# Sums of the down weights formed in the first up projection, with loads and stores on GpSimd's queue

## The chip, the cores and the metric

The kernel runs on one core of a Trainium2 chip. The metric is the device time of one execution in microseconds (us), and each change is judged by the ratio of the medians of timed runs. The engines are named as in the profile: PE is TensorE (matmuls; PEld its weight loads), DVE is VectorE, ACT is ScalarE, POOL is GpSimd, SP is SyncE, whose queue carries most DMA transfers.

## The reference

Two transformer blocks run one after the other on x of 1024 tokens by 1024 features, in float32. Each ends with a feed-forward part of 2816 hidden features:

```
gate, up = jnp.split(xn @ w_gate_up, 2, axis=-1)            # first block
x = x + (jax.nn.silu(gate) * up) @ w_down

u = causal_dwconv(h @ w_ffn_up, w_ffn_conv)                 # second block
gate, val = jnp.split(u, 2, axis=-1)
x = x + (jax.nn.silu(gate) * val) @ w_ffn_down
```

The change is in these two parts. What lies ahead of them (attention, gating, delta rule, short convolutions) is not touched.

## The kernel before

**Precision.** Each float32 operand is split into a high part (ScalarE casts it, line 256) and a low part (VectorE subtracts the high part, line 257). A product is three matmuls: high x high, high x low, low x high.

**Up projection** (`unit`, line 1061). One pass of Strassen's scheme in Winograd's form replaces eight block products by seven. A unit `f` (1 to 21) makes 128 gate and 128 up features: 84 matmuls of 128x512. Its weights come as two raw blocks `wr` and go through four slots (`add_unit`), in which the sums S1 to S4 of weight blocks are formed in place: S3 and S4 on VectorE, S1 and S2 on GpSimd (table `SE`). `unit` copies the first product out of PSUM into a buffer `u` on ScalarE (line 1072); the results go to DRAM as `hd`, feature by feature, through the buffer `sg`.

**Down projection** (`strassen` in `ffn`, line 1231). The same scheme over 20 of the 22 hidden blocks, as two halves of ten: seven products of 10 steps each (`DOWN`: A11 B11, A12 B21, S3 T3, A22 T4, S1 T1, S2 T2, S4 B22), so 70 steps of 12 matmuls. A is the hidden activations read back from `hd`, B the down weights. The two blocks left over go through `down`, which in the first block stands ahead of product S2. Operand `i` is split into one of `AR` = 3 ring buffers `ah` (`operand`), and its sums of A blocks are formed at the same place. B11, B12 and B21 lie whole in SBUF, B22 comes twice through `wr`, and `add_down` forms T1 to T4 from them in the slots: T3 and T1 on VectorE, T2 and T4 on GpSimd (line 845).

**Order.** Each engine works through its instructions in order. A list scheduler sets that order: it may move instructions ahead that it takes to be ready, and operands are issued with a priority (`PR["op"]`). `Weights` keeps up to two raw blocks loaded and three slots split ahead of TensorE; it works through its slots in the order in which they were added.

Of the kernel before, what the change touches and what calls it, by code (L numbers as in the profile page):

```python
# [8 lines left out]
F32 = mybir.dt.float32  # L9
# [9 lines left out]
P = 128  # L19
# [33 lines left out]
DE = dict(S3=pool_, T3=vec_, T1=vec_, T2=pool_, T4=pool_, S1=vec_, S2=vec_, S4=pool_)  # L53
# [104 lines left out]
class Kern:  # L158
# [6 lines left out]
    def setup(self):  # L165
# [5 lines left out]
        self.hd = self.dram.tile([NF, P, S], F32, name="hd")  # L171
        self.ident = c.tile([P, P], F32, name="ident")
# [643 lines left out]
    def plan_ffn(self, which):  # L816
# [5 lines left out]
        for f in range(1, NF):  # L822
            units[f] = self.add_unit(*[up[:, :, o + f * P:o + (f + 1) * P] for o in (0, DFF)])
# [6 lines left out]
        for _, name in DOWN:  # L830
            if which == 1 and name == "T2":
                rest()
            for k in range(0, ND, 2):
                slots[name, k] = self.add_down(home, name, k, dn)
# [4 lines left out]
    def add_down(self, home, name, k, dn):  # L839

        W, nc = self.W, self.nc
        raw = W.load([(0, dn[:, ND + k:ND + k + 2, 512:])], 2, 512) if name in ("T3", "B22") else None

        def tt(out, in0, in1, what):
            DE[what](nc).tensor_tensor(out=out, in0=in0, in1=in1, op=ALU.subtract)  # L845

        def make(hi, lo):
            out = []
            for j in range(2):
                h, l = (v[:, j * 512:(j + 1) * 512] for v in (hi, lo))  # L850
                b11, b12, b21 = (home.get((q, k + j)) for q in ("B11", "B12", "B21"))
                b22 = None if raw is None else W.raw[raw][:, j * 512:(j + 1) * 512]
                if name == "T3":
                    src = home["T3", j]
                    tt(src, b22, b12, "T3")
                    tt(b12, b12, b11, "T1")
                    tt(b11, b22, b12, "T2")
                else:
                    src = dict(B11=b11, B21=b21, T4=b21, T1=b12, T2=b11, B22=b22)[name]
                    if name == "T4":  # L860
                        tt(b21, b21, b11, "T4")
                self.split(h, l, src)
                out.append((h, l))
            return out
        return W.slot(make, raw)

    def add_unit(self, gate, up):
# [9 lines left out]
        def tt(name, in0, in1, op, what):  # L877
            SE[what](nc).tensor_tensor(out=raw(name), in0=raw(in0), in1=raw(in1), op=op)  # L878
# [63 lines left out]
    def ffn(self, which):  # L942
# [118 lines left out]
        def unit(f):  # L1061
# [32 lines left out]

            if f < NF - 1:
                second()
                third()
# [16 lines left out]
            add(u2[:, main], b5, u2[:, main])  # L1114
            if f == NF - 1:
                down_open()
# [19 lines left out]
        def fetch(q, k0, k1):  # L1136

            f = k0 + ND * ((q[2] if q[0] == "A" else q[1]) == "2")
            c = 512 * ((q[1] if q[0] == "A" else q[2]) == "2")
            src = self.hd[f:f + k1 - k0, :, c:c + 512].rearrange("k p c -> p k c") if q[0] == "A" else \  # L1140
                dn[:, f:f + k1 - k0, c:c + 512]
# [9 lines left out]
        def down_load():  # L1151

            for q, part in (("A11", "hi0"), ("B11", "lo0")):
                place(q, self.xnp.tile([P, KT, 512], F32, tag=part, name=q), 0, KT)
            for k in range(0, KT, 2):
                fetch("A11", k, k + 2)
                fetch("B11", k, k + 2)
# [1100 lines left out]
```

## Time and profile before

| what | value |
|---|---|
| median of 3 runs | 2544.11 us (2541.62 to 2544.75) |
| the profiled execution | 2533.62 us |
| its span, first to last instruction | 2531.9 us |
| busy over the span | PE 96%, DVE 73%, ACT 45%, POOL 18% |
| mean granted TensorE clock | 0.986 of full |

The shares are averages over all stages. Where TensorE stands still, and for whom, has to be read stage by stage; the stages of the change lie at 545 to 949.5 us (first up projection), 949.5 to 1189.5 (first down projection, dn1), 1866 to 2285 (second up projection) and 2285.5 to 2524 (second down projection, dn2).

### The profile page before, as it was taken

To read this page: it belongs to the slowest core of one execution; us is meant where nothing else is said; L and a number is where in the kernel's file an instruction comes from. 1 tells how busy PE (TensorE), PEld (TensorE's weight loads), DVE (VectorE), ACT (ScalarE), POOL (GpSimd) and SP (SyncE) were. 2 spreads that over 40 slices of the span, in tenths; PEclk is the share of its full clock that TensorE was granted. 3 is DMA by queue.
4 is the path that set the end of the run, shared out by engine and by line. 5 is a ranking of instruction groups with operands and counts; after the bars stand their busy time and mean duration, and the time that the engine had idled before them with its cause. 6 is when DMAs were issued, how large, how long until landed. Compare 5 with 4: busy or idle time off the path is not lost. (4 is left out here: it accounts for less than half of the span.)

```text
span 2531.9 us, 33317 instructions
## 1 busy us (share of the span) xinstructions
PE 2420.6 (96%) x12360; PEld 1993.5 (79%) x12360; DVE 1856.3 (73%) x3342; ACT 1145.8 (45%) x2290; POOL 449.3 (18%) x412
## 2 busy tenths in 40 slices
PE   7999999999999999899999999989899999999898
PEld 7977779978888887678877777879678888887677
DVE  5557788655555557977777868777878788878977
ACT  5356675342232233337432434776744434434243
POOL 1000002031111114500210111332341111113600
PEclk9999999999999999899999999999999999999999
DMA  4110002112223236213211112131212222227202
GB/s 152 51 34 21 22 26 92 42 48 78 75 83 91 76 110 240 75 42 123 62 42 50 30 46 64 40 137 49 75 51 84 92 75 75 84 93 265 67 33 109
DMA packets 194675, 196.58 MB, mean 78 GB/s; under 512 B 11613, under 2 KB 154032, under 8 KB 194512
## 3 DMA queue, kind: packets, MB, share of 16 engines
q1 hardware_dynamic: 189760, 178.74, 22.2%
q0 software_dynamic: 4752, 15.71, 1.8%
q8 instruction: 97, 1.59, 0.3%
q14 instruction: 66, 0.54, 0.1%
HBM read 155.76 MB, written 38.67 MB: 77 GB/s over the span
## 5 line engine op out<-in xcount | busy, mean ns | idle before, releaser
L257 DVE TENSOR_TENSOR wl<-wr,wh 128x512 fp32r<-128x512 f32 (+4 forms) x388 | 300.9, 805 | 320.1 <-ACT wh L256 316.2
L256 ACT CAST wh<-wr 128x512 fp32r<-128x512 f32 (+4 forms) x388 | 257.2, 696 | 583.4 <-PE st L973 363.9
L269 PE MATMUL dn<-wh,ah 128*128 128x512 f32 x560 | 225.6, 403 | 21.6 <-DVE ah L257 21.6
L267 PE MATMUL dn<-wh,ah 128*128 128x512 f32 x560 | 226.0, 404 | 5.4 <-ACT ah L256 2.2
L268 PE MATMUL dn<-wl,ah 128*128 128x512 f32 x560 | 224.0, 400 | 0.0
L980 DVE TENSOR_TENSOR u<-st,u 128x512 f32<-128x512 f32 x260 | 168.0, 685 | 30.7 <-PE st L973 29.3
L878 POOL TENSOR_TENSOR wr<-wr 128x512 f32<-128x512 f32 x42 | 55.2, 1315 | 692.3 <-DVE wr L878 692.3
L269 PEld LDWEIGHTS dn<-wh,ah 128*128 128x128 f32 x560 | 107.3, 192 | 56.3 <-DVE ah L257 30.8
L973 PE MATMUL st<-f1hi,wl 128*128 128x512 f32 x368 | 147.2, 400 | 0.0
L973 PE MATMUL st<-f2hi,wl 128*128 128x512 f32 x368 | 147.1, 400 | 0.0
L973 PE MATMUL st<-f2lo,wh 128*128 128x512 f32 x368 | 147.0, 400 | 0.0
L973 PE MATMUL st<-f1lo,wh 128*128 128x512 f32 x368 | 146.6, 398 | 0.0
L973 PE MATMUL st<-f1hi,wh 128*128 128x512 f32 x368 | 145.2, 394 | 0.7 <-ACT f1hi L256 0.7
L973 PE MATMUL st<-f2hi,wh 128*128 128x512 f32 x368 | 145.0, 394 | 0.7 <-ACT f2hi L256 0.7
L267 PEld LDWEIGHTS dn<-wh,ah 128*128 128x128 f32 x560 | 107.4, 192 | 32.8 <-ACT ah L256 4.1
L268 PEld LDWEIGHTS dn<-wl,ah 128*128 128x128 f32 x560 | 107.5, 192 | 24.0
L256 ACT CAST ah<-A 128x512 fp32r<-128x512 f32 x104 | 63.7, 619 | 109.7 <-PE dn L268 94.7
L257 DVE TENSOR_TENSOR ah<-A,ah 128x512 fp32r<-128x512 f32 x104 | 82.4, 796 | 41.9 <-ACT ah L256 38.9
L973 PEld LDWEIGHTS st<-f2hi,wh 128*128 128x128 f32 x368 | 70.4, 191 | 17.3 <-ACT f2hi L256 0.9
L973 PEld LDWEIGHTS st<-f1hi,wh 128*128 128x128 f32 x368 | 70.4, 191 | 17.2 <-ACT f1hi L256 0.9
L973 PEld LDWEIGHTS st<-f2lo,wh 128*128 128x128 f32 x368 | 69.6, 189 | 16.0
L973 PEld LDWEIGHTS st<-f1lo,wh 128*128 128x128 f32 x368 | 69.4, 189 | 16.1
(547 smaller groups left out, 7079.8 us busy)
## 6 DMA issues: line engine op xcount, KB each, us to landing
wr<-in_w_gate_up_dram SPq DMA_DIRECT2D x44, 512.0 KB, 4.3
hd<-sg SPq DMA_DIRECT2D x44, 512.0 KB, 3.2
wr<-in_w_ffn_up_dram SPq DMA_DIRECT2D x44, 512.0 KB, 3.9
wr<-in_w_mix_in_dram SPq DMA_DIRECT2D x28, 512.0 KB, 4.0
wr<-in_w_in_dram SPq DMA_DIRECT2D x16, 512.0 KB, 3.9
wr<-in_w_down_dram SPq DMA_DIRECT2D x12, 512.0 KB, 3.3
wr<-in_w_ffn_down_dram SPq DMA_DIRECT2D x12, 512.0 KB, 3.3
A<-hd SPq DMA_DIRECT2D x4, 1280.0 KB, 14.3
```

Source lines behind the costliest of these rows:

```text
L256: self.nc.scalar.copy(hi, src)
L257: self.nc.vector.tensor_tensor(out=lo, in0=src, in1=hi.bitcast(F32), op=ALU.subtract)
L267: mm(out, a[0], b[0], start=start, stop=False)
L268: mm(out, a[0], b[1], start=False, stop=False)
L269: mm(out, a[1], b[0], start=False, stop=stop)
L878: SE[what](nc).tensor_tensor(out=raw(name), in0=raw(in0), in1=raw(in1), op=op)
L973: mm(ps, a[p][:, kk, :], b[q][:, kk, :], start=start and kk == 0 and j == 0, stop=kk == n - 1 and j == 2, skip_group_check=True)
L980: nc.vector.tensor_tensor(out=out, in0=ps, in1=t, op=ALU.add)
```

## The change

- The sums T1 to T4 of both down projections are formed during the first up projection. `prepare_down` goes over 20 blocks (10 of each set of weights): four loads of 128x512 from DRAM, four GpSimd sums, four stores to new DRAM tensors `td`, all on GpSimd's queue. It is a generator which `unit` advances three times, so a unit takes one block. A GpSimd copy of one column from the unit's first result into each load's buffer (`self.now`) ties the loads to the unit.
- In the down projections all seven B operands (four of them from `td`) come through `wr` as blocks of 512 KB for two steps; B11, B12 and B21 no longer lie in SBUF. The loop's own A sum S2 moves from VectorE to GpSimd (`DE`).
- In the first up projection S1 and S2 of the weights move from GpSimd to VectorE (`SE[1]`); in the second they stay.
- The ring of A operands has six buffers, three of them opened when the up projection's pool is released.

```
-ND, AR, A2, PB = 10, 3, 2, 2
+ND, AR, AR0, A2, PB = 10, 6, 3, 2, 2
-SE, TE, ME = dict(S3=vec_, S1=pool_, S2=pool_, S4=vec_), dict(T1=vec_, T2=pool_, T3=pool_, T4=pool_), vec_
+SE = {1: dict(S3=vec_, S1=vec_, S2=vec_, S4=vec_), 2: dict(S3=vec_, S1=pool_, S2=pool_, S4=vec_)}
-DE = dict(S3=pool_, T3=vec_, T1=vec_, T2=pool_, T4=pool_, S1=vec_, S2=vec_, S4=pool_)
+DE = dict(S3=pool_, S1=vec_, S2=pool_, S4=pool_)
...
+    def add_down(self, which, name, k, dn):
+        f, c = k + ND * (name[1] == "2"), 512 * (name[2:] == "2")
+        return self.W.add([(0, dn[:, f:f + 2, c:c + 512] if name[0] == "B" else self.td[which, name][:, k:k + 2, :])],
+                          2, 512)
+    def prepare_down(self, pool):
+        nc = self.nc
+        for which in (1, 2):
+            dn = self.ffn_plan[which][3]
+            for k in range(ND):
+                def load(name):
+                    f, c = k + ND * (name[1] == "2"), 512 * (name[2] == "2")
+                    t = pool.tile([P, 512], F32, tag="pb", name="pb", bufs=6)
+                    nc.gpsimd.tensor_copy(t[:, 0:1], self.now)
+                    nc.gpsimd.dma_start(out=t, in_=dn[:, f, c:c + 512])
+                    return t
+                def keep(name, out, in0, in1, op):
+                    nc.gpsimd.tensor_tensor(out=out, in0=in0, in1=in1, op=op)
+                    nc.gpsimd.dma_start(out=self.td[which, name][:, k, :], in_=out)
+                b12, b22, b11, b21 = (load(n) for n in ("B12", "B22", "B11", "B21"))
+                yield
+                keep("T3", b22, b22, b12, ALU.subtract)
+                keep("T1", b12, b12, b11, ALU.subtract)
+                yield
+                keep("T2", b11, b11, b22, ALU.add)
+                keep("T4", b21, b21, b11, ALU.subtract)
+                yield
...
             nc.scalar.copy(p1[:, main], b1)
+            self.now = p1[:, 2:3]
...
+            next(prep, None)
             if f < NF - 1:
                 second()
+                next(prep, None)
                 third()
...
+            next(prep, None)
             if f == NF - 1:
                 down_open()
...
-            d2 = tc.alloc_tile_pool(name=f"dr{which}", bufs=1, side="right", reuse_waits="tile")
-            dp.append(d2)
+            d = tc.alloc_tile_pool(name=f"dr{which}", bufs=1, side="right", reuse_waits="tile")
+            dp.append(d)
+            ring["ah"] += [d.tile([P, 2, 512], F32R, name=f"ah{i}") for i in range(AR0, AR)]
...
+            for i in range(AR0, AR):
+                operand(i)
```

Three places show how the order moves. The first is GpSimd in the first up projection. Before, it has the two sums S1 and S2 of each unit in the raw blocks `wr`:

```order
L878 TENSOR_TENSOR wr_5970<-wr_5970 128x512 [waits DMAHW2_49,DVE_49,Activation_49]
L878 TENSOR_TENSOR wr_5970<-wr_5970,wr_6053 128x512 [waits DMAHW3_49,Activation_49,Pool_49]
L878 TENSOR_TENSOR wr_6118<-wr_6118 128x512 [waits DMAHW4_49,DVE_49,Activation_49]
L878 TENSOR_TENSOR wr_6118<-wr_6118,wr_6159 128x512 [waits DMAHW6_49,Activation_49,Pool_49]
L878 TENSOR_TENSOR wr_6254<-wr_6254 128x512 [waits DMAHW0_49,DVE_49,Activation_49]
L878 TENSOR_TENSOR wr_6254<-wr_6254,wr_6295 128x512 [waits DMAHW1_49,Activation_49,Pool_49]
```

With the change it has a block of `prepare_down` per unit, here the first one (`pb` are its buffers, `td1T` the DRAM tensors of the first down projection; waits on DMASW are for transfers of its own queue):

```order
L860 COPY pb<-u 128x1 x3
L861 DMA pb<-in_w_down_dram 128x512 [waits DMASW5_49,Pool_49]
L861 DMA pb<-in_w_down_dram 128x512 [waits DMASW6_49,Pool_49]
L861 DMA pb<-in_w_down_dram 128x512 [waits DMASW7_49,Pool_49]
L861 DMA pb<-in_w_down_dram 128x512 [waits DMASW0_49,Pool_49]
L865 TENSOR_TENSOR pb<-pb 128x512 [waits DMASW6_49,DMASW5_49]
L866 DMA td1T_69<-pb 128x512 [waits DMASW1_49,Pool_49]
L865 TENSOR_TENSOR pb<-pb 128x512 [waits DMASW7_49]
L866 DMA td1T_67<-pb 128x512 [waits DMASW2_49,Pool_49]
L865 TENSOR_TENSOR pb<-pb 128x512
L866 DMA td1T_68<-pb 128x512 [waits DMASW3_49,Pool_49]
L865 TENSOR_TENSOR pb<-pb 128x512 [waits DMASW0_49]
```

The sums on `wr` have gone to VectorE, and eight transfers have come.

The second is ScalarE at the start of the first down projection. Before, the rows begin after operands 0 to 2 have been cast, with weight casts (`wh`) and the next operands in the order of the steps (three buffers `ah`):

```order
L256 CAST wh_8838<-B_8777 128x512 [waits DMAHW5_49,DVE_49,PE_49]
L256 CAST wh_8838<-B_8777 128x512
L241 ACTIVATE sg<-u 128x512 [waits DVE_49]
L256 CAST ah_8851<-A_8776 128x512 [waits PE_49,Activation_49]
L256 CAST ah_8852<-A_8776 128x512 [waits DMAHW4_49,PE_49,Activation_49]
L256 CAST wh_8932<-B_8777 128x512 [waits DMAHW7_49,PE_49]
L256 CAST wh_8932<-B_8777 128x512
L256 CAST ah_8853<-A_8776 128x512 [waits PE_49,Activation_49]
```

With the change, the first row is operand 2; the second set of three buffers (`ah_9284` to `ah_9286`) holds operands 3 to 5, and the first set takes operands 6, 7 and 8 (`A11x`):

```order
L260 CAST ah_9256<-A_9184 128x512 [waits DMAHW1_49]
L260 CAST wh_9241<-wr_9219 128x1024 [waits DMAHW4_49,DVE_49,PE_49]
L245 ACTIVATE sg<-u 128x512 [waits DVE_49]
L260 CAST ah_9254<-A_9184 128x512 [waits DMAHW3_49,PE_49,Activation_49]
L260 CAST ah_9255<-A_9184 128x512 [waits PE_49,Activation_49]
L260 CAST wh_9332<-wr_9226 128x1024 [waits DMAHW6_49,PE_49]
L260 CAST ah_9256<-A11x 128x512 [waits DMAHW5_49,PE_49,Activation_49]
L260 CAST ah_9284<-A_9184 128x512 [waits DMASW3_49,DMASW2_49,DMASW4_49,DMASW1_49,Pool_49]
L260 CAST ah_9285<-A_9184 128x512 [waits DMAHW2_49,DMASW3_49,DMASW2_49]
L260 CAST ah_9286<-A_9184 128x512 [waits DMASW3_49]
L260 CAST ah_9284<-A11x 128x512 [waits DVE_49,PE_49]
```

Operands 6, 7 and 8 stand ahead of 3, 4 and 5; the one of step 8 waits for PE to leave its buffer, which holds step 2.

The third is VectorE in the second down projection, where the product S3 T3 is made ready. Before, T3 (`T`) and T1 (`B_20253`) stand among the subtractions of operands (`ah`) and weights (`wl`):

```order
L845 TENSOR_TENSOR T_20244<-wr_20076,B_20253 128x512
L845 TENSOR_TENSOR T_20245<-wr_20076,B_20253 128x512
L257 TENSOR_TENSOR ah_20239<-A_20237,ah_20239 128x512
L257 TENSOR_TENSOR wl_20553<-B_20291,wh_20552 128x512 x2
L845 TENSOR_TENSOR B_20253<-B_20253,B_20164 128x512
L257 TENSOR_TENSOR ah_20240<-A_20237,ah_20240 128x512
L845 TENSOR_TENSOR B_20253<-B_20253,B_20164 128x512
L980 TENSOR_TENSOR x<-dn,x 128x512 x2
L257 TENSOR_TENSOR ah_20238<-A_20237,ah_20238 128x512
L257 TENSOR_TENSOR wl_20593<-T_20244,wh_20592 128x512
```

With the change the same place has only the subtractions, of weights that were read as sums, and the sums into x:

```order
L261 TENSOR_TENSOR ah_20610<-A_20497,ah_20610 128x512
L261 TENSOR_TENSOR wl_20921<-wr_20845,wh_20920 128x1024
L261 TENSOR_TENSOR ah_20611<-A_20497,ah_20611 128x512
L261 TENSOR_TENSOR ah_20612<-A_20497,ah_20612 128x512
L261 TENSOR_TENSOR wl_20959<-wr_20885,wh_20958 128x1024
L261 TENSOR_TENSOR ah_20567<-A_20497,ah_20567 128x512
L990 TENSOR_TENSOR x<-dn,x 128x512 x4
L261 TENSOR_TENSOR ah_20568<-A_20497,ah_20568 128x512
L261 TENSOR_TENSOR wl_20995<-wr_20924,wh_20994 128x1024
L261 TENSOR_TENSOR ah_20569<-A_20497,ah_20569 128x512
```

The VectorE sums of line 845 are gone, and so are those on GpSimd.

## Rows read from the trace of the kernel before

**Rows 1.** Windows of four stages: us, busy us by engine, clock, DMA share, GB/s.

```profile
core 0: us, PE busy (x) PEld busy (x) DVE busy (x) ACT busy (x) POOL busy (x), PEclk, DMA share, GB/s
...
545.00:949.50 404.50, 404.46 (x1743) 328.67 (x1742) 219.92 (x348) 117.21 (x207) 51.70 (x40) 1.00 0.29 86
949.50:1110.00 160.50, 147.71 (x601) 114.98 (x600) 138.77 (x180) 59.65 (x103) 69.52 (x42) 0.96 0.39 141
...
1866.00:2285.00 419.00, 419.00 (x1808) 340.62 (x1807) 338.85 (x510) 175.45 (x324) 51.82 (x40) 1.00 0.26 85
2285.50:2410.00 124.50, 111.71 (x457) 86.52 (x455) 114.44 (x150) 46.58 (x82) 64.86 (x38) 0.97 0.43 157
...
```

**Rows 2.** Tile dn, dn1 then dn2: ns min/median/max, first and last start.

```profile
L267 PE MATMUL dn<-wh,ah x280: 387/397/628, 949.5 to 1189.0; 128*128 128x512 f32 x140
L267 PE MATMUL dn<-wh,hh x32: 388/394/395, 1110.1 to 1131.5; 128*128 128x512 f32 x32
...
L267 PE MATMUL dn<-wh,ah x280: 387/397/628, 2285.5 to 2501.6; 128*128 128x512 f32 x140
L267 PE MATMUL dn<-wh,hh x32: 388/394/395, 2502.3 to 2523.7; 128*128 128x512 f32 x32
```

**Rows 3.** Timeline of TensorE in dn1 and dn2: start us, us.

```profile
949.54 0.39 PE L267 MATMUL dn<-wh,ah 128*128 128x512 f32 x1
...
955.94 0.40 PE L268 MATMUL dn<-wl,ah 128*128 128x512 f32 x1
...
2354.01 0.63 PE L268 MATMUL dn<-wl,ah 128*128 128x512 f32 x1
2354.44 0.63 PE L269 MATMUL dn<-wh,ah 128*128 128x512 f32 x1
```

**Rows 4.** Waits of TensorE, dn1 then dn2: total us, times, longest us.

```profile
PE dn L269 <- DVE ah L257: 10.9, 8, 2.8
...
PE dn L269 <- DVE ah L257: 10.7, 8, 2.9
```

**Rows 5.** Groups by line and shape, 945 to 1150: busy, mean ns, idle before.

```profile
L257 DVE TENSOR_TENSOR wl<-B,wh 128x512 fp32r<-128x512 f32 x44 | 35.8, 853 | 2.9 <-ACT wh L256 2.8
...
L845 POOL TENSOR_TENSOR B<-wr,B 128x512 f32<-128x512 f32 x8 | 18.1, 2261 | 11.6 <-DVE B L845 9.7 <-ACT ah L256 1.9
```

**Rows 6.** The same view of the first up projection, 545 to 950.

```profile
L257 DVE TENSOR_TENSOR wl<-wr,wh 128x512 fp32r<-128x512 f32 x141 | 92.6, 692 | 165.0 <-ACT wh L256 164.2
L256 ACT CAST wh<-wr 128x512 fp32r<-128x512 f32 x141 | 81.6, 618 | 251.8 <-PE st L973 212.3 <-DMA wr<-in_w_gate_up_dram 36.2 <-POOL wr L878 3.4
...
L878 POOL TENSOR_TENSOR wr<-wr,wr 128x512 f32<-128x512 f32 x20 | 25.9, 1294 | 1.6
```

**Rows 7.** Timeline of GpSimd, then VectorE, in dn2.

```profile
2338.33 6.05 POOL L845 TENSOR_TENSOR B<-wr,B 128x512 f32<-128x512 f32 x1
...
2356.58 1.71 POOL L845 TENSOR_TENSOR B<-wr,B 128x512 f32<-128x512 f32 x1
...
2355.40 1.77 DVE L257 TENSOR_TENSOR wl<-T,wh 128x512 fp32r<-128x512 f32 x1
```

**Rows 8.** DMAs issued by line 2141 on GpSimd's queue; their stretch's window.

```profile
L2141 POOL DMA_DIRECT2D xnd<-xs x4: 531/593/604, 1803.2 to 1819.1; - x4
...
DMA to landing us min/median/max: 3.0/3.1/5.7
...
1798.00:1820.00 22.00, 14.50 (x58) 9.03 (x57) 21.38 (x42) 14.64 (x28) 7.72 (x8) 0.80 0.23 89
```

**Rows 9.** Timeline of ScalarE in the first up projection.

```profile
718.59 0.59 ACT L1072 COPY u<-st 128x512 f32<-128x512 f32 x1 [1.27 <-PE st L973]
738.07 0.59 ACT L1072 COPY u<-st 128x512 f32<-128x512 f32 x1 [1.27 <-PE st L973]
```

**Rows 10.** Timeline at dn2's start: TensorE, then the SP queue.

```profile
2289.36 0.50 PE L267 MATMUL dn<-wh,ah 128*128 128x512 f32 x1 [1.61 <-DVE u L980]
...
2296.80 0.33 SPq L1059 DMA_DIRECT2D hd<-sg  x1
```

More of the change, by code (lines that the diff above doesn't have):

```diff
@@ L171, in setup @@
         self.hd = self.dram.tile([NF, P, S], F32, name="hd")
+        self.td = {(w, n): self.dram.tile([P, ND, 512], F32, name=f"td{w}{n}")
+                   for w in (1, 2) for n in ("T1", "T2", "T3", "T4")}
         self.ident = c.tile([P, P], F32, name="ident")
@@ L822, in plan_ffn @@
         for f in range(1, NF):
-            units[f] = self.add_unit(*[up[:, :, o + f * P:o + (f + 1) * P] for o in (0, DFF)])
+            units[f] = self.add_unit(which, *[up[:, :, o + f * P:o + (f + 1) * P] for o in (0, DFF)])
         home, slots = {}, {}
@@ L833, in plan_ffn @@
             for k in range(0, ND, 2):
-                slots[name, k] = self.add_down(home, name, k, dn)
+                slots[name, k] = self.add_down(which, name, k, dn)
         if which == 2:
@@ L837, in plan_ffn @@
         self.ffn_plan[which] = (units, home, slots, dn, dw)
[L839 to L865, printed above, removed]
@@ L869, in add_unit @@
+    def add_unit(self, which, gate, up):
         W, nc = self.W, self.nc
@@ L877, in tt @@
         def tt(name, in0, in1, op, what):
-            SE[what](nc).tensor_tensor(out=raw(name), in0=raw(in0), in1=raw(in1), op=op)
+            SE[which][what](nc).tensor_tensor(out=raw(name), in0=raw(in0), in1=raw(in1), op=op)
         def cut(hi, lo, *names):
@@ L1151, in down_load @@
         def down_load():
-            for q, part in (("A11", "hi0"), ("B11", "lo0")):
-                place(q, self.xnp.tile([P, KT, 512], F32, tag=part, name=q), 0, KT)
+            place("A11", self.xnp.tile([P, KT, 512], F32, tag="hi0", name="A11"), 0, KT)
             for k in range(0, KT, 2):
                 fetch("A11", k, k + 2)
-                fetch("B11", k, k + 2)
         ring = {}
@@ L1165, in down_open @@
             place("A12", d.tile([P, ND, 512], F32, name="A12"), 0, ND)
-            ring["ah"] = [d.tile([P, 2, 512], F32R, name=f"ah{i}") for i in range(AR)]
+            ring["ah"] = [d.tile([P, 2, 512], F32R, name=f"ah{i}") for i in range(AR0)]
             d = tc.alloc_tile_pool(name=f"dm{which}", bufs=1, reuse_waits="tile")
             dp.append(d)
-            for j in range(2):
-                home["T3", j] = d.tile([P, 512], F32, name=f"T3{j}")
             ring["a22"] = [d.tile([P, 512], F32, name=f"a22{i}") for i in range(A2)]
-            for q in ("A11", "B11", "A21", "B12"):
+            for q in ("A11", "A21"):
                 place(q, d.tile([P, ND - KT, 512], F32, name=f"{q}x"), KT, ND)
-            for q, part in (("A21", "hi1"), ("B12", "lo1")):
-                place(q, self.xnp.tile([P, KT, 512], F32, tag=part, name=q), 0, KT)
+            place("A21", self.xnp.tile([P, KT, 512], F32, tag="hi1", name="A21"), 0, KT)
             fetch("A11", KT, ND)
-            fetch("B11", KT, ND)
             fetch("A12", 0, ND // 2)
             fetch("A12", ND // 2, ND)
-            for i in range(AR):
+            for i in range(AR0):
                 operand(i)
@@ L1233, in strassen @@
             last = None
[L1234 to L1235 removed]
+            d = tc.alloc_tile_pool(name=f"dr{which}", bufs=1, side="right", reuse_waits="tile")
+            dp.append(d)
+            ring["ah"] += [d.tile([P, 2, 512], F32R, name=f"ah{i}") for i in range(AR0, AR)]
             self.psum(dn=(1, 8))
[L1237 to L1241 removed]
+            for k0, k1 in ((0, KT // 2), (KT // 2, KT), (KT, ND)):
+                fetch("A21", k0, k1)
             for k in range(A2):
                 load22(k)
+            for i in range(AR0, AR):
+                operand(i)
             sums = []
@@ L1259, in strassen @@
                     banks = [self.bank(tag="dn", name="dn") for _ in range(4)]
-                w = W.get(slots[bname, k - k % 2])[k % 2]
+                w = [v[:, k % 2, :] for v in W.get(slots[bname, k - k % 2])]
                 a = ready.pop(i)
@@ L1282, in strassen @@
                 W.done(slots[DOWN[-1][1], ND - 2])
+                dp.pop(1).release()
             return last
@@ L1287, in ffn @@
         pool = tc.alloc_tile_pool(name=f"ffn{which}", bufs=1, side="right", reuse_waits="tile")
+        prep = self.prepare_down(pool) if which == 1 else iter(())
         first(banks)
@@ L1300, in ffn @@
             down(range(2 * ND, NF), self.tail2())
-            dp[1].release()
+            for d in dp[:0:-1]:
+                d.release()
     def tail1(self):
```

14 lines of the change are left out of this document (3 added, 11 removed).

## The prediction

> **What bounds the kernel now.** I read the busy time by stage first, because the share over the whole span (TensorE 96%) hides where it waits. [Rows 1] has the four stages the change touches. In the first and the second up projection TensorE is busy for all of the stretch (404.46 of 404.5 us, 419.00 of 419) at a granted clock of 1.00: nothing done beside them can make them shorter, only longer. In the first part of each down projection it is not: 147.71 of 160.5 us and 111.71 of 124.5 us, at a granted clock of 0.96 and 0.97, so some of the busy time is slow too. That is where there is time to win.
>
> How much? A step of a down projection is 12 matmuls. Two of them 28 apart start at 949.54 and 955.94 [rows 3], so at the full level (2.4 GHz) one takes 0.2286 us and a step 2.74 us. In the first down projection (dn1 below; the second is dn2) the 50 steps ahead of the two left-over blocks run from 949.5 to 1110.1 [rows 2]: 160.6 us for 600 matmuls that need 137.2, so **23.4 us** are lost. In dn2 all 70 steps run from 2285.5 to 2502.3: 216.8 us for 840 matmuls that need 192.0, so **24.8 us** are lost. Together 48.2 us; the rest of the two stages runs at full pace (so the last 20 steps of the first, whose end also holds tail work, are left out).
>
> Who makes TensorE wait? The chain of waits of these stretches says nearly always the same: the matmul of line 269, which needs the low part of an A operand, waits for the VectorE subtraction of line 257, 8 times and 10.9 and 10.7 us in total [rows 4]. The remainder up to 23 us is the clock: behind such a wait matmuls follow each other by 0.43 us instead of 0.23 [rows 3] (1.2 GHz), after TensorE had stood idle for two or three us.
>
> Why is VectorE late? In that stretch of dn1 it is busy 138.77 of 160.5 us, and its instructions there are longer than elsewhere: the same subtraction of 128x512 takes 853 ns on average in the first down projection [rows 5] and 692 in the up projection [rows 6]. The timeline shows how [rows 7]: while GpSimd forms T2 and T4 (line 845, 1.7 us each, one took 6.05), VectorE's subtractions take 1.77. One VectorE instruction of 0.69 and one GpSimd sum of 1.3 take 1.7 to 1.8 together: they take turns.
>
> **The change, step by step.** (1) *Both down projections* lose ten T3 and ten T1 on VectorE and ten T2 and ten T4 on GpSimd each, and the loads of B11, B12 and B21 in big pieces. Two of the four A sums change engine as well: S2 goes to GpSimd. Per projection VectorE sheds 30 instructions of 0.69 (20 B sums, 10 S2), 21 us, and GpSimd 20 of 1.7 to 2.3 [rows 5, 7] less the ten S2 it takes. What is left for VectorE per step is two subtractions (2 x 0.69), in places a sum for x or S1 (0.69 each): 1.4 to 2.8 us against 2.74 for TensorE. And six operands wait ready in place of three, 16.5 us of work in place of 8.2. So the long waits of the middle should go.
>
> What is late next? Three places. *Step 3.* The order on ScalarE shows that steps 6, 7 and 8 (issued with priority as steps 0 to 2 are consumed) are split ahead of step 3, and step 8 waits until TensorE is done with step 2. So TensorE always stops there once. In dn1 step 2 ends at 949.5 + 36 x 0.2286 = 957.7; then come two casts of 0.62 [rows 6] and a subtraction of 0.69: **2 us**. In dn2 it is longer, as VectorE still has the last convolution: its last product is stored at 2296.80 [rows 10], and behind it come the subtractions of step 7, of two weight blocks (2 x 0.69), of step 8 and step 3: 3.4 us, to 2300.2, where TensorE, which starts again at 2289.36 with 27 matmuls of steps 0 to 2 to go and has two of step 3 that need only the high part, wants it at 2296.0. That is 4 us, and 1.6 for eight matmuls at the lower clock behind it: **5.5 us**. *The start of dn2* keeps most of its wait of 1.61 us [rows 10]: **1 us**. *The A22 product*: GpSimd now has two sums per step there (S2, S4), 2.6 us at 1.29 [rows 6] or 3.4 at 1.7 [rows 7] against a step of 2.74; over eight steps between a lead of 1 us and a lag of 5, and the three more operands cover 8. I keep **2 us** each (0 to 5). Left over: 2 + 2 and 5.5 + 1 + 2, together 12.5; won: 48.2 - 12.5 = **35.7 us**.
>
> (2) *The weight loads in the down projections* become one stream of 512 KB per two steps, 5.5 us. Slots are three deep and raw buffers two, so a load issued as its buffer comes free is wanted two slots, 11 us, later, and a transfer of that size lands in 3.0 to 5.7 [rows 8]. I charge nothing; what covers it is the two slots already split, and without them each late load would cost what it is late.
>
> (3) *The first up projection* gets all the work that was removed. A unit takes 19.48 us (738.07 - 718.59, [rows 9]). VectorE: two sums more per unit, 40 x 0.69 = 28 us, to 248 of 404.5; if all 80 GpSimd sums of 1.3 shut it out, 352, or 87%. In the second up projection VectorE has 338.85 and GpSimd 51.82 of 419, 93%, and TensorE never waits [rows 1]. So the cover is there; without it each unit would lose what VectorE has above 19.48 us. DMA: 160 transfers of 256 KB, 42 MB, bring 86 GB/s at a busy share of 0.29 to about 190 at 0.64; the row of ScalarE's casts says what that may cost: it waits 212.3 us for TensorE to free a slot and 36.2 for weights to land [rows 6], and TensorE for neither. I charge **1 us**.
>
> (4) *GpSimd's block per unit* is the price that nothing in the trace shows whole: four copies of one column, four loads, four sums, four stores. An issue takes 0.53 to 0.60 us, also where VectorE is busy 21.38 of 22 us, and lands 3.0 to 5.7 later [rows 8]; a sum takes 1.29 to 2.26 [rows 5, 6]; a copy of one column lies between nothing and an issue. Low: two issues 1.1, the landing 3.0, then four sums and stores 4 x (1.3 + 0.55): 11.5 us. High: 2.4 + 1.2 + 5.7 + 4 x (2.26 + 0.60): 20.7. I take 14, nearer the low end, since the two sums that GpSimd now has in a unit of this very stage take 1.29 with VectorE busy 54% beside them. Below 19.48 it costs nothing: only ScalarE's copy into `u` of the next unit waits for it, a unit later. The Trainium skill has a rule against transfers on this queue ("SBUF — State Buffer", the section SBUF: two separate sides): while VectorE holds the port that it shares with GpSimd, GpSimd cannot write descriptors, and a DMA of 0.62 us takes some 3.1; it advises another queue. By that rule, if it held for all eight issues, a block would be an estimated 14 + 8 x 2.5 = 34 us and the kernel 290 us slower; by the rows above, 0.53 to 0.60 beside a busy VectorE, nothing.
>
> Sum: 35.7 - 1 = 35 us. The profiled execution took 2533.62 us, 10 less than the median of the runs, 2544.11; I take the difference off the median: **2509 us**.
>
> **Rivals.** *GpSimd cannot do a block per unit.* Then ScalarE's copy waits for it, everything behind that copy on ScalarE too (the casts of weights), and TensorE for these: 20 x (block - 19.48). At the high bound, 20.7, the time is 2533; from 21.2 us on the whole gain is gone; with one sum in each block held up to 6.05 us, as one was [rows 7], on top of the high bound, the block is 24.5 and the time 2609. For it: that row. Against it: it stood where VectorE had no gap, and here VectorE is idle 46% of the time now and 39% with its two sums more. 8%.
> *The up projection loses a little per unit* (weights land late beside 2 MB more per unit, or VectorE's subtractions come late by a GpSimd sum of 1.3): 1 us in each of 20 units gives 2529. 12%.
> *The wait moves within the down projections:* GpSimd's two sums per step in A22, or SP's queue, where weights now stand behind loads that wait for a free buffer, bring back half: 2527. For it: S2 now holds the buffers of A22. 18%.
> *Likeliest*, 62%: 2509, its own range 2499 to 2521 (12.5 left over may be 4 or 22).
>
> **Numbers.** What can be told from no change is 0.2%, 5 us. Faster: all of the likeliest and of the third rival, most of the second, 0.87. Same 0.05. Slower, the first rival with the tail of the second, 0.08. The range is 2497 (nearly all of the loss gone) to 2532, which takes in the second and third rival and leaves out the first.
>
> **What would show it.** Right: 600 and 840 matmuls of dn1 and dn2 in about 142 and 201 us; line 269's wait once per stage near step 3 and hardly elsewhere; VectorE's 128x512 subtractions in the down projections near 0.7; the up projection with TensorE still busy throughout and GpSimd idle for some us of each unit until ScalarE's copy lets it go. Wrong: `u` on ScalarE waiting for GpSimd in the up projection, units longer than 19.5 us, or waits for `a` or `wr` in the middle of the down projections.

## The result, and the profile with the change

The changed kernel takes **2676.07 us** (median of four runs, 2673.15 to 2680.9) against 2542.86 us before: 1.054 times as long, 95% interval 1.0518 to 1.0563. The prediction said 2509.

The windows of the four stages, in the form of [rows 1], say at once where. First up projection, first part of dn1, second up projection, first part of dn2:

```profile
core 0: us, PE busy (x) PEld busy (x) DVE busy (x) ACT busy (x) POOL busy (x), PEclk, DMA share, GB/s
545.00:1108.00 563.00, 451.78 (x1750) 358.64 (x1748) 301.41 (x388) 118.80 (x208) 201.98 (x320) 0.88 0.41 138
1111.00:1255.50 144.50, 141.56 (x599) 113.34 (x600) 117.89 (x123) 57.06 (x80) 53.45 (x31) 0.99 0.48 159
2020.00:2444.00 424.00, 423.22 (x1832) 343.87 (x1833) 343.27 (x514) 178.53 (x329) 54.35 (x42) 1.00 0.26 84
2444.20:2569.00 124.80, 118.70 (x495) 94.78 (x494) 112.51 (x118) 51.66 (x72) 51.94 (x30) 0.97 0.51 170
```

The first up projection, of which TensorE was busy every moment before, takes 563 us in place of 404.5. TensorE stands still in a fifth of it, and its clock is at 0.88 of full. The first row explains the whole result; the down projections did become shorter. Their first and last matmuls, as in [rows 2]:

```profile
L271 PE MATMUL dn<-wh,ah x280: 387/396/628, 1110.9 to 1334.7; 128*128 128x512 f32 x140
L271 PE MATMUL dn<-wh,hh x32: 392/397/398, 1255.8 to 1277.4; 128*128 128x512 f32 x32
...
L271 PE MATMUL dn<-wh,ah x280: 387/396/632, 2444.2 to 2648.5; 128*128 128x512 f32 x140
L271 PE MATMUL dn<-wh,hh x32: 392/394/397, 2649.2 to 2670.7; 128*128 128x512 f32 x32
```

The 50 steps of dn1 take 1255.8 - 1110.9 = 144.9 us (160.6 before), the 70 of dn2 take 205.0 (216.8): 27.5 us won. The spans differ by 2679.0 - 2531.9 = 147.1 us: 157.6 in the units of the first up projection, 0.8 ahead of them, 3.0 between the last matmul of the up projection and the first of dn1, 3.0 behind the last of dn1, less 27.5 in the two products; the other 10.2 lie in stages that the change does not touch. They come from the execution of before that was profiled, which was 9 us faster than the median: with the same code there as before, the last experiment below took 9 us longer between dn1 and the second up projection.

Who makes TensorE wait in the up projection? The waits from 560 to 1060, all engines (us in total, times, longest):

```profile
ACT wh L260 <- DMA wr<-in_w_gate_up_dram: 128.4, 15, 9.4
...
POOL pb L860 <- ACT u L1082: 199.4, 18, 11.8
...
PE st L983 <- DVE u L990: 104.5, 18, 7.0
```

TensorE waits for a VectorE sum, once in each unit, 5.8 us on average. GpSimd waits too: 11 us in each unit for ScalarE's copy `u`, that is, it has done its block well before the next one may start. So the prediction's first rival (GpSimd cannot do a block per unit) is not what happened. ScalarE waits 128 us for weights to land.

### The profile page after: what moved, and what is told of

It is laid out like the page before. It is cut to its first block, busy times and chain, and to the rows that moved or that the text cites. A ratio compares the mean times of both kernels' runs of the same rounds, so it can differ in the third digit from the quotient of the medians.

```text
span 2679.0 us, 33648 instructions
## 1 busy us (share of the span) xinstructions
PE 2466.3 (92%) x12360; PEld 2030.3 (76%) x12360; DVE 1906.1 (71%) x3254; ACT 1139.9 (43%) x2220; POOL 564.0 (21%) x670
## 5 line engine op out<-in xcount | busy, mean ns | idle before, releaser
L261 DVE TENSOR_TENSOR wl<-wr,wh 128x512 fp32r<-128x512 f32 (+3 forms) x438 | 422.6, 988 | 424.5 <-ACT wh L260 420.8
L260 ACT CAST wh<-wr 128x512 fp32r<-128x512 f32 (+3 forms) x438 | 319.1, 755 | 807.0 <-PE st L983 362.0
L983 PE MATMUL st<-f1hi,wh 128*128 128x512 f32 x368 | 165.5, 450 | 111.2 <-DVE u L990 109.2
L983 PEld LDWEIGHTS st<-f1hi,wh 128*128 128x128 f32 x368 | 80.7, 220 | 138.0 <-ACT sg L245 117.0
L983 PE MATMUL st<-f1lo,wh 128*128 128x512 f32 x368 | 162.0, 440 | 0.0
L983 PE MATMUL st<-f1hi,wl 128*128 128x512 f32 x368 | 161.1, 438 | 0.0
L865 POOL TENSOR_TENSOR pb<-pb 128x512 f32<-128x512 f32 x80 | 103.3, 1291 | 95.9 <-DMA pb<-in_w_down_dram 49.2
L261 DVE TENSOR_TENSOR ah<-A,ah 128x512 fp32r<-128x512 f32 x104 | 84.6, 826 | 35.8 <-ACT ah L260 35.7
L888 POOL TENSOR_TENSOR wr<-wr 128x512 f32<-128x512 f32 x21 | 27.2, 1294 | 346.4 <-DVE wr L888 346.4
L983 PEld LDWEIGHTS st<-f1lo,wh 128*128 128x128 f32 x368 | 80.5, 219 | 18.3
L983 PEld LDWEIGHTS st<-f1hi,wl 128*128 128x128 f32 x368 | 79.2, 215 | 19.1
```

What stands on the lines that cost most here:

```text
L260: self.nc.scalar.copy(hi, src)
L261: self.nc.vector.tensor_tensor(out=lo, in0=src, in1=hi.bitcast(F32), op=ALU.subtract)
L865: nc.gpsimd.tensor_tensor(out=out, in0=in0, in1=in1, op=op)
L888: SE[which][what](nc).tensor_tensor(out=raw(name), in0=raw(in0), in1=raw(in1), op=op)
L983: mm(ps, a[p][:, kk, :], b[q][:, kk, :], start=start and kk == 0 and j == 0, stop=kk == n - 1 and j == 2, skip_group_check=True)
```

## One unit, before and after

TensorE's products of a unit, in order, are A11 B11 and A22 T4 (weights from slot a), S1 T1 and S3 T3 (slot b), S2 T2 and A12 B21 (slot c), and S4 B22 (slot d), 12 matmuls each. `u2` and `v` are VectorE's first two sums of a unit's results; both write buffers `u`.

To see why a sum is late, follow what it waits for. Here is one unit with the change, by the timeline (start us, us), TensorE, ScalarE, SP's queue, VectorE, GpSimd:

```profile
722.89 0.76 PE L983 MATMUL st<-f1hi,wh 128*128 128x512 f32 x1 [5.45 <-DVE u L990]
730.47 0.39 PE L983 MATMUL st<-T4h,wh 128*128 128x512 f32 x1
750.47 0.77 PE L983 MATMUL st<-f1hi,wh 128*128 128x512 f32 x1 [5.90 <-DVE u L990]
...
727.69 1.14 ACT L260 CAST wh<-wr 128x512 fp32r<-128x512 f32 x2 [5.00 <-PE st L983]
733.26 0.62 ACT L260 CAST wh<-wr 128x512 fp32r<-128x512 f32 x1 [1.88 <-PE st L983]
742.63 1.14 ACT L260 CAST wh<-wr 128x512 fp32r<-128x512 f32 x2 [8.75 <-DMA wr<-in_w_gate_up_dram]
...
734.63 24.11 SPq L130 DMA_DIRECT2D wr<-in_w_gate_up_dram  x2
...
743.28 2.37 DVE L261 TENSOR_TENSOR wl<-wr,wh 128x512 fp32r<-128x512 f32 x2 [8.68 <-ACT wh L260]
745.58 2.22 DVE L888 TENSOR_TENSOR wr<-wr,wr 128x512 f32<-128x512 f32 x1
747.84 0.69 DVE L888 TENSOR_TENSOR wr<-wr 128x512 f32<-128x512 f32 x1
748.44 0.68 DVE L990 TENSOR_TENSOR u<-st,u 128x512 f32<-128x512 f32 x1
749.04 0.68 DVE L888 TENSOR_TENSOR wr<-wr,wr 128x512 f32<-128x512 f32 x1
749.64 1.88 DVE L990 TENSOR_TENSOR u<-st,u 128x512 f32<-128x512 f32 x3
...
731.97 2.13 POOL L861 DMA_DIRECT2D pb<-in_w_down_dram  x4
743.80 1.30 POOL L865 TENSOR_TENSOR pb<-pb 128x512 f32<-128x512 f32 x1
745.97 1.27 POOL L865 TENSOR_TENSOR pb<-pb 128x512 f32<-128x512 f32 x1
```

The first and the last TensorE row are the first matmul of S4 B22 in two units: it adds to a bank that `v`, the first of the three sums at 749.64, has to read first. On VectorE `v` stands behind `u2` (748.44), and both stand behind the split of slot a of the *next* unit (743.28) and its S3 and S1. That split waits for weights that were issued at 734.63, when the split of slot d had freed their buffer. Slot d (733.26) waits until TensorE has done both products of slot a, and slot c (727.69), split ahead of it, until TensorE has done the S4 B22 of the unit before. So it is a **loop that closes once in a unit**. The same places in a unit of before:

```profile
712.81 0.40 PE L973 MATMUL st<-f1hi,wh 128*128 128x512 f32 x1
732.33 0.39 PE L973 MATMUL st<-f1hi,wh 128*128 128x512 f32 x1
...
715.64 1.14 ACT L256 CAST wh<-wr 128x512 fp32r<-128x512 f32 x2 [1.16 <-PE st L973]
721.18 0.62 ACT L256 CAST wh<-wr 128x512 fp32r<-128x512 f32 x1 [2.00 <-PE st L973]
727.54 1.14 ACT L256 CAST wh<-wr 128x512 fp32r<-128x512 f32 x2 [5.74 <-DMA wr<-in_w_gate_up_dram]
...
718.98 3.94 SPq L129 DMA_DIRECT2D wr<-in_w_gate_up_dram  x2
...
729.40 0.68 DVE L878 TENSOR_TENSOR wr<-wr,wr 128x512 f32<-128x512 f32 x1
730.00 3.21 DVE L980 TENSOR_TENSOR u<-st,u 128x512 f32<-128x512 f32 x5
730.73 0.69 DVE L980 TENSOR_TENSOR u<-st,u 128x512 f32<-128x512 f32 x1
```

(Merged rows give the first start and the time to the last end; the second of the two loads at 718.98 is issued at 722.55, an issue taking 0.37. The last row is `v`, the second of the five sums, in a window of its own.) Piece by piece; a piece ends where the next one starts, and `v` with its end:

| piece of the loop, us | before | with the change |
|---|---|---|
| S4 B22 on TensorE, until slot c is cast | 2.83 | 4.80 |
| slots c and d, until slot d is cast | 5.54 | 5.57 |
| cast and split of slot d, until the weights are issued | 1.37 | 1.37 |
| the weights, until slot a is cast | 4.99 | 8.00 |
| cast and `wl` of slot a | 1.86 | 2.95 |
| S3 | 0.60 | 2.26 |
| S1 (GpSimd's before) | - | 0.60 |
| `u2`, S2 (GpSimd's before), `v` | 1.42 | 1.88 |
| left until TensorE starts S4 B22 | 0.91 | 0.15 |
| sum | 19.52 | 27.58 |

The unit before had 0.9 us to spare, and few units had much more: in two thirds of them `v` ends 1.16 us before TensorE needs it and `u2` has waited 0.4 for TensorE ahead of that, 1.6 in all. The change adds in four of the pieces. Weights land 3.0 us later: GpSimd's four loads (1 MB, 731.97 to 734.1) and the store of `hd` are issued in the same four us as the two weight loads. The Trainium skill says as much ("DMA: Bandwidth & Descriptors", section Issuing engines are not separate DMA queues: transfers started by different engines run interleaved on the same 16 DMA engines), and the 8.00 us beside 4.99 agree. `wl` and S3 are 2.7 us longer and fall beside GpSimd's sums at 743.80 and 745.97. S1 and S2 are 1.2 us more in the same queue. And the stall itself makes the loop longer: behind it the 24 matmuls from 722.89 to 730.47 take 7.58 us, since at first they follow each other by 0.43 us (the lower level, 1.2 GHz). At the full level 24 take 5.5; 2.0 of the difference are inside the loop.

## The experiments

Times are medians; "before" ran beside each set (2538 to 2544 us). The length of the first up projection, from 545 us to its last matmul, is in the text (before 404 us, with the change 562). The expectations, quoted as they were written ahead of each run, set three accounts against each other. Theory A adds up what the change put into the stretch from the weight loads to `v`. Rival B holds the transfers alone to be the cause, rival C VectorE's work alone.

**1. No preparation at all.**

```
...
-        prep = self.prepare_down(pool) if which == 1 else iter(())
+        prep = iter(())
```

> Leaves out the whole preparation in the first up projection (no loads, sums or stores on GpSimd); the down projections read plain weight blocks in place of T1 to T4, so the output is not the reference's. S1 and S2 of the weights stay on VectorE. Theory A (one chain per unit from the weight loads to VectorE's sum u2: landing later by 3.1 us, VectorE's wl and S3 longer by 2.6 us beside GpSimd's sums, S1 and S2 in the same queue 1.3 us, less a cover of 1.5 us): 1.3 alone is covered, the first up projection is back at 404 us and the time is 2676 - 157 = 2519 us. Rival B (the transfers alone): the same 2519. Rival C (VectorE alone, by its two sums more and the shared port): the sums alone cost something, 20 x 1 to 3 us, so 2540 to 2580. This run also gives what the down projections won by themselves.

2521.48 us, ratio 0.9935 (0.9913 to 0.9956); the up projection takes 405 us. The two sums on VectorE by themselves fit into the spare time (`v` now ends some 0.5 us before TensorE needs it), so VectorE's two sums are not the cause by themselves. It also gives what the down projections are worth by themselves: 17 us, not 35.

**2. Transfers without sums.**

```
-                    nc.gpsimd.tensor_tensor(out=out, in0=in0, in1=in1, op=op)
                     nc.gpsimd.dma_start(out=self.td[which, name][:, k, :], in_=out)
```

> Leaves out GpSimd's four sums of each block; its loads and stores stay (what is stored are unsummed weights, so the output is not the reference's). Theory A: the landing (3.1 us) and VectorE's two sums (1.3) stay, less 1.5 of cover, 2.9 us of stall per unit and 2.1 of low clock behind it: 20 x 5 = 100 us lost of 157, 2619 us. Rival B (transfers alone): nearly nothing changes, 2660 to 2680. Rival C (VectorE alone): most is won back, 2520 to 2545.

2618.0 us, ratio 1.0314 (1.0289 to 1.034), up projection 500 us. TensorE still waits for the same sum (line numbers one lower), a little over half as long:

```profile
PE st L982 <- DVE u L989: 58.1, 19, 4.5
```

A's number holds; both the transfers alone (B) and VectorE alone (C) are out. Of a unit's two weight loads it is the second that slot a waits for; it lands after 7.4 us here (median), as with the change, and after 3.9 before.

**3. The block 11 us later.**

```
-            self.now = p1[:, 2:3]
...
                 third()
+                self.now = u2[:, 2:3]
+                next(prep, None)
```

> The block of a unit starts 11 us later: the copy of one column reads u2 (VectorE's first sum of the unit) and no longer the first product's copy, so the four loads come after the weights of the next unit have landed; GpSimd's sums then lie 7 to 16 us behind u2, ahead of the next wl and S3, but its stores fall beside the next weight loads. Theory A: VectorE's 2.6 us go, and the landing decides: at 4.4 us as before no loss, 2520; at 6 us 1.4 us of stall and 2.1 of low clock per unit, 2590. Rival B (transfers alone, whenever they are): 2620 to 2670, since as many bytes move in each unit. Rival C: 2520 to 2545.

2606.1 us, ratio 1.0264 (1.0238 to 1.029), up projection 497 us. That is above both of A's ends and below B's. Over all weight loads the landing took 4.9 us (median), but the second one of a unit, for which slot a waits, took 6.05. For 6 us A's sum gave 2590, so it lacked some 16 us. TensorE waited 56.6 us.

**4. S1 and S2 back on GpSimd.**

```
-SE = {1: dict(S3=vec_, S1=vec_, S2=vec_, S4=vec_), ...
+SE = {1: dict(S3=vec_, S1=pool_, S2=pool_, S4=vec_), ...
```

> S1 and S2 of the up weights go back to GpSimd, where they stand behind the block of the unit. Theory A: 1.3 us of the chain go, 4.2 of stall and 2.1 of low clock stay, 20 x 6.3 = 126 us of 157: 2645 us. Rival B: no change, 2676. Rival C: 2580. If GpSimd's order (S1 behind the whole block of 15 us) makes slot b late, it is slower than 2676 instead, and the wait of TensorE is then for the weights of S1.

2620.31 us, ratio 1.0332 (1.0302 to 1.0363), up projection 517 us: more came back than A said (56 us, not 31), and TensorE still waits for the sum `u`, not for S1's weights. Why A was 25 us out is not shown. The first down projection started with no wait.

**5. The block behind the landing of the next weights.**

```
-            self.now = p1[:, 2:3]
...
                 second()
+                self.now = W.parts[units[f + 1][0]][0][0][:, 0, 0:1]
                 next(prep, None)
```

> The whole work of the change stays, but a unit's block starts when the weights of the next unit have landed: its copy of one column reads the high part of the next unit's A11, which ScalarE casts behind the landing. Theory A: the four loads and most stores then lie where no weight load is under way, so the landing is back near 4.3 us, GpSimd's sums start some 4 us behind wl and S3 and do not lengthen them, and of the three terms only S1 and S2 (1.3 us, under the cover of 1.5) are left: the first up projection takes 405 to 412 us, the time is that of e1_no_prep, 2521 (2515 to 2535). Rival B (it is the amount that is moved in each unit, 3.5 MB, wherever it lies): weights late again, 2590 to 2640.

2607.78 us, ratio 1.0266 (1.0247 to 1.0284), up projection 494 us. This fits B's number and not A's. `wl` and S3 of slot a had their short durations again, as A wanted. But GpSimd's sums had moved beside the split of slot c of the same loop, on VectorE, where two subtractions take 4.43 us in place of 1.3. S4 and the cast of slot d stand behind them; that cast is at 737.02, 7.7 us after slot c's (729.30), where it was 5.6:

```profile
721.87 1.29 DVE L261 TENSOR_TENSOR wl<-wr,wh 128x512 fp32r<-128x512 f32 x2 [6.66 <-ACT wh L260]
723.08 0.69 DVE L888 TENSOR_TENSOR wr<-wr,wr 128x512 f32<-128x512 f32 x1
...
730.31 4.43 DVE L261 TENSOR_TENSOR wl<-wr,wh 128x512 fp32r<-128x512 f32 x2
```

And the store of `hd` and both weight loads, spread over 4.2 us before (718.34, 718.98, 722.55), now come within 1.8 on SP's queue, so that the last needs 5.9 us to land with no load of GpSimd's beside it:

```profile
713.49 0.37 SPq L130 DMA_DIRECT2D wr<-in_w_gate_up_dram  x1
714.24 0.34 SPq L1069 DMA_DIRECT2D hd<-sg  x1
715.24 22.12 SPq L130 DMA_DIRECT2D wr<-in_w_gate_up_dram  x2
```

**Theory A falls** in this form. Its terms are in the trace, but it was a sum over one stretch, from the weight loads to `v`; the work that is moved out of that stretch meets the same loop in another.

**6. Sums without transfers.** GpSimd's four sums on buffers of zeros, started by the same cast as in 5.

```
-                    nc.gpsimd.dma_start(out=t, in_=dn[:, f, c:c + 512])
...
-                    nc.gpsimd.dma_start(out=self.td[which, name][:, k, :], in_=out)
```

> No loads and no stores on GpSimd, but its four sums per unit stay, on buffers that hold zeros, and start at the same cast, so that they lie beside VectorE's wl and S3 of the next unit, as they did with the change (the down projections read plain weights, the output is not the reference's). Theory A: landing as before; 2.6 us of longer wl and S3 and 1.3 of S1 and S2 less the cover of 1.5 give 2.4 us of stall, 2.1 of low clock behind it, 20 x 4.5 = 90 us: 2521 + 90 = 2611. Rival B (the transfers alone): 2521.

2557.85 us, ratio 1.0065 (1.0043 to 1.0087), up projection 443 us: a third to a half of A's loss, but not B's nothing. No transfer of GpSimd's is left here, and the weights still land after 5.1 us in the median. TensorE waits 26.4 us for `u`. It is the split of slot b that is longer here (two subtractions 3.04 us, with slot c's behind them), not slot a's, and `hd` and the weight loads stand within 2.1 us of each other as in 5. So both kinds of work cost. Above the 2521 of experiment 1, the transfers at the change's place cost 97 of 155 us, and the sums at the place of experiment 5 cost 36 of 86; sums alone at the change's place were not run. That the spare time of the loop lets the first delay off cheaply, and none behind it, fits these numbers and is not shown by itself.

**7 and 8. Buffers in the down projections**, on top of 5.

```
-ND, AR, AR0, A2, PB = 10, 6, 3, 2, 2
+ND, AR, AR0, A2, PB = 10, 3, 3, 2, 2        # 7
+ND, AR, AR0, A2, PB = 10, 5, 3, 4, 2        # 8
```

> e5_after_landing with three operands ahead in the down projections in place of six. If the ring is worth what the prediction gave it (16.5 us of work ready in place of 8.2), the waits for line 261 in the product A22 T4 come back and it is over 5 us slower than e5_after_landing; if the stall at step 3 is most of what the ring does, 7 us come back and it is as fast or up to 7 us faster.

> e5_after_landing with four buffers for the blocks of A22 in place of two, paid for by five operands ahead in place of six. If the waits of about 4.5 us in each A22 product come from the two buffers that GpSimd's S2 holds, 5 to 9 us faster than e5_after_landing; if they come from VectorE and GpSimd taking turns there (two sums per step), no change beyond 3 us.

2605.86 and 2601.6 us (ratios 1.0258 and 1.024, beside 1.0266 for experiment 5). With three operands ahead the stall at step 3 is gone and waits of 1.4 us for line 261 come in the product A22 T4, one for the other: dn1 and dn2 take 145.7 and 204.6 us against 144.3 and 205.0. With four buffers for A22 its waits are gone altogether, so those waits came from the two buffers; five operands in place of six cost part of it back at step 3 of dn2 (142.4 and 203.9 us). The median is 6.2 us below that of experiment 5, inside the 5 to 9 expected, but the two products account for only 3.0 of it.

**Theory D: the loop as a whole.** If TensorE waits because `u2` and `v` stand behind slot a of the next unit, it should be enough to put them ahead of it. TensorE then needs slot a only for A11 B11, one product later, and three of the pieces leave the loop. The order alone is changed:

```
-                if f < NF - 1:                     # in second()
-                    W.done(sb)
...
-                add(v[:, main], b5, u2[:, main])
+                self.vadd = add(v[:, main], b5, u2[:, main]).ins
+                W.done(sb)
...
                 ins = self.split(x, y, raw(name))  # slot a
+                if behind:
+                    self.tc.add_manual_dep(ins.ins, behind.name, NOSYNC, reason="order of the unit")
```

Here `behind` is `self.vadd`, the sum `v`.

> The whole work of the change stays; VectorE's two sums u2 and v, for which TensorE waits, are put ahead of wl of the next unit's slot a in VectorE's order (an ordering alone, no wait is taken away). Theory D (a loop that closes within a unit: TensorE ends S4 B22, then slot c is split, slot d, the weights are loaded into the buffer that comes free, slot a of the next unit is split, u2 and v follow it on VectorE, TensorE starts the next S4 B22; 27.6 us long with the change against 19.5 of TensorE's work): with the sums ahead, TensorE needs slot a only for A11 B11, behind S4 B22, so the loop is shorter by S3, S1, u2, S2 and v (4.7 us of the trace) and by one product (2.7) and its low clock: from 27.6 to about 19, no stall or one of under 1 us per unit, 2520 to 2545 us. Rival E (the weights cannot be brought and split at this pace, wherever VectorE has its sums): 2600 or more, and TensorE waits for wl of slot a in place of u.

> e9_adds_first with the block of e5_after_landing (it starts when the next unit's weights have landed). Theory D: 2520, within 10 us of e9_adds_first, since neither stalls. Rival E: 2590 to 2610.

> e9_adds_first with S1 and S2 of the up weights back on GpSimd, behind its block. Theory D: S1 behind a block of 15 us makes slot b late: 2530 to 2580; TensorE starts the first down projection without the wait of 2.8 us for a sum u (3 us). Rival E: 2600 or more.

**9.** 2541.28 us, ratio 1.0002 (0.999 to 1.0014), up projection 431 us. All loads, sums and stores of the change are still there, at the same place in a unit, and the second weight load of a unit still lands after 7.9 us (median): 135 of the 155 us were the order. What is left is the wait that E named, in D's size (15 us between 560 and 940):

```profile
PE st L985 <- DVE wl L261: 10.8, 16, 1.6
PE st L985 <- ACT wh L260: 4.1, 5, 1.4
```

**10** (9 with the start of the block from 5). 2519.08 us, ratio 0.9912 (0.989 to 0.9934): faster than before by 23 us, and inside the prediction's range. It is D's 2520, but not within 10 us of experiment 9, which still stalls. With the block behind the landing the loop closes in time, and TensorE waits for nothing. The windows of the up projection and the two down projections:

```profile
545.00:951.00 406.00, 406.00 (x1751) 330.16 (x1750) 309.38 (x389) 123.11 (x208) 242.46 (x320) 1.00 0.57 190
951.00:1096.50 145.50, 141.01 (x602) 112.10 (x601) 118.27 (x128) 57.38 (x80) 51.43 (x31) 1.00 0.51 170
2280.80:2405.00 124.20, 119.04 (x504) 95.07 (x503) 112.19 (x119) 51.38 (x72) 53.03 (x30) 0.99 0.52 171
```

190 GB/s, VectorE busy 76% and GpSimd 60% of the up projection, and TensorE 100% at full clock: the resources were there, as the prediction had counted them. E falls, and so does the form of B in which the amount moved per unit counts wherever it lies. The weights land after 4.2 us in the median, as before.

**11** (the edit of 4 on top of 9). 2559.96 us, ratio 1.0065 (1.0041 to 1.0088), up projection 446 us, within D's bounds. The weights land after 8.8 us (median of the stretch from 560 to 940), and TensorE waits 22.6 us for the casts and `wl` of weights, which fits D's account of S1 behind GpSimd's block. dn1 starts without a wait, but so it does in 9 and 10.

**12. The order of experiment 9 in the kernel before**, by the same edit.

> The kernel before with the one edit of e9_adds_first (u2 and v ahead of wl of the next unit's slot a on VectorE), nothing else of the change. Theory D: before, the loop is shorter than TensorE's 19.48 us per unit and TensorE never waits, so to shorten it brings nothing: within 5 us of before, and the 157 us that the edit, with the block moved, gives back belong to the loop alone. If the order itself is worth something, it is 5 to 20 us faster than before, and e10_adds_first_landing owes its gain partly to it.

2538.49 us against 2544.49, ratio 0.9982 (0.9966 to 0.9997): at most a few us; the medians differ by 6.0, a little over D's 5. In the two profiled executions the up projections, from their first to their last matmul, take 449.8 us before and 448.8 with the order exchanged, so the order gives at most 1 us there, and dn1 and dn2 do not gain either (161.1 and 216.3 us against 160.6 and 216.8). What else makes the medians differ is not shown. Experiment 10's gain lies where the change was to bring it: its dn1 and dn2 take 145.5 and 202.5 us.

## Why the prediction was wrong

**The step that failed is (3)**, the up projection: "the cover is there", "I charge 1 us". It measured 157.6. The cover was read from shares (VectorE 87% at most, DMA 0.64) and from ScalarE's 212.3 us of waiting for TensorE. None of these numbers was false, and experiment 10 shows the same resources doing the same work in 406 us. But a share says how much room there is in a stage, not at which place, and a long wait for TensorE does not say how early the weights were. At slot a's cast they were not early: the cast at 707.27 waits 4.92 us for TensorE, and its weights, issued at 703.10, landed at 706.96, 0.3 us ahead of it. In seven casts the weights came last, and these are the 36.2 us of [rows 6]. The row of the cast at 707.27 in the trace of before:

```profile
707.27 1.14 ACT L256 CAST wh<-wr 128x512 fp32r<-128x512 f32 x2 [4.92 <-PE st L973]
```

What decided was the spare time of one sum, 0.9 us in the unit shown, and it stood in the trace of before: `v` ends at 731.42 and TensorE starts at 732.33. A wait of zero was taken for a cover without asking how far from a wait it was. The second up projection, taken as proof that VectorE and GpSimd may be 93% busy together, has no GpSimd block and 85 GB/s.

**Rival by rival.** The likeliest case fell with (3). "The up projection loses a little per unit" named both mechanisms, weights that land late and subtractions late by a GpSimd sum, and priced them at 1 us; with the loop closing they cost 7.9, stall and clock. "GpSimd cannot do a block per unit" pointed this way (2609 at most) and had not this cause: the block takes some 16 us of 27 (16.7 in the unit shown, 731.44 to 748.1; 14 was predicted) and GpSimd then waits. Its loads land after 4.3 to 8.4 us, where 3.0 to 5.7 was predicted. "The wait moves within the down projections" was partly right (below).

**GpSimd's queue (4).** The rule of the Trainium skill that was weighed there ("SBUF — State Buffer", section SBUF: two separate sides) would have had the issues wait while VectorE holds the port. They did not: all 80 loads were issued in 538 to 585 ns and all 80 stores in 549 to 562, so the trace is with the rows. The rule itself is not refuted by that, since the section states it for VectorE operations in a 2-port mode, a condition that the prediction left out. The same section says of the port that one of the two engines blocks and they do not share. `wl` and S3 fit that: 2.22 us for a sum of 0.69 beside one of 1.3. That the one that starts first keeps the port, as it also says, these rows do not bear out: S3 starts at 745.58 and GpSimd's sum at 745.97, and S3 is the long one (starts of GpSimd's rows are rough).

**The down projections (1)** won 27.5 us in their products where 35.7 were expected, and lost 6 beside them. Of the 8.2 missing, 4.5 are the product A22 (below) and some 4 the pace: the prediction counted 0.2286 us for a matmul, but the 120 of A12 B21 in dn2, where TensorE waits for nothing, take 27.78 us, 0.2315 each, so less than 48.2 us was there to be won. The waits of TensorE with the change, dn1 and then dn2:

```profile
PE dn L271 <- DVE u L990: 2.8, 1, 2.8
PE dn L272 <- DVE wl L261: 1.8, 1, 1.8
PE dn L271 <- ACT ah L260: 1.0, 1, 1.0
...
PE dn L272 <- DVE wl L261: 2.6, 1, 2.6
PE dn L273 <- DVE ah L261: 1.9, 1, 1.9
PE dn L271 <- ACT ah L260: 1.0, 1, 1.0
PE dn L271 <- DVE u L990: 0.5, 1, 0.5
```

The middle is free, as forecast: [rows 4] had eight waits in each. Step 3 was right in place and size: steps 2 and 3 take 1.8 us too long in dn1 (2 predicted) and 5.1 in dn2 (5.5), the start of dn2 1.0 (1). A22 was too small: 4.0 and 4.5 us with the low clock behind it, where 2 each were kept out of 0 to 5; experiment 8 puts it on the two buffers. Two things were not foreseen: dn1 starts 3 us late, behind VectorE's last sums of the up projection (gone in experiment 4, where S1 and S2 are GpSimd's, and in 9, where the order alone is exchanged), and the tail of dn1 is 3 us longer, as TensorE now finishes ahead of the sums into x.

**Weight loads in the down projections (2)** at nothing: no wait for `wr` shows among TensorE's, as said.

**What stays open:** how the 155 us divide between transfers, sums and the two moved sums (97 for transfers with S1 and S2, 0 for S1 and S2 alone; the sums were measured only at another place). A third raw buffer, which would break the loop at the weight loads, was not tried, for lack of room.

## What to carry to other kernels

Before work is put "under" a stage that an engine bounds, follow one period of its pipeline round and add up the pieces: the difference to the period is the cover, and shares and zero waits do not show it. Here it was 0.9 to 1.6 us of 19.5 in most units, while VectorE stood idle 46% of the time. Where an engine works in order, look what the result that the bounding engine waits for stands behind: a sum behind work for the next period ties the two together, and to exchange them was worth 135 us, more than any way of placing the added work. And such a loop punished delays twice here: behind a stall of over 5 us the clock was low, and that made the loop 2.0 us longer.

## What the runs showed of the hardware that was not expected

- Weights of 512 KB land in 4.3 us (median, before; 3.9 for the second load of a unit), in 7.9 in the unit shown, where 1 MB on GpSimd's queue and two more transfers of 512 KB were issued in the same four us, and in 5.9 where only the latter two stood within 1.8 us of it (experiment 5).
- VectorE's subtractions of 128x512 took 0.69 us each, and up to 2.3 beside GpSimd's sums, while GpSimd's own stayed at 1.27 to 1.32 in all 80 of the changed kernel: there it was VectorE that paid. In experiment 10 it was GpSimd: its first sum of a block took 2.4 to 3.2 in 15 of 20 blocks, and VectorE's instructions beside the one at 719.68 (3.08 us) kept their 0.69.
- A GpSimd copy of one column of `u` takes 0.18 us (median of the 80 with the change), the first of a block up to 0.73; of a column of `wh`, as in experiment 5, 0.66. An issue takes 0.55.
